# One decoder layer on one core: a raw transposed copy of x kept in DRAM from the first stage, inverse roots in pairs, and two smaller edits

## The chip, the cores and the metric

The kernel runs on one core of a Trainium2 chip. The metric is the device time of one execution in microseconds (us), taken as the median of repeated runs; the profile is one further execution with the hardware profiler on, and has a time of its own.

## The reference, cut to what matters

One layer of a hybrid decoder is computed for 1024 prompt tokens and 8 sampled tokens (T = 1032 rows in all, tiled as 8 tiles of 128 rows and a ninth of 8). What the change touches is the first norm and projection, the residual, and the one-token update of the delta state of the sampled tokens:

```
xn = rms_norm(x, norm_mix);  h = xn @ w_in          # first stage: norm, then projections
...
x = x + jnp.sum(gates * proj, axis=2) @ w_out       # x here is the raw input: the residual
hn = rms_norm(x, norm_ffn); ...
# sampled tokens (one step), per head and request:
S = exp(g) * (I - beta k k^T) S + beta k v^T        # an outer product is added to S
```

## The kernel before, in words

Everything is done in one launch, by five engines with queues of their own: TensorE (PE), VectorE (DVE), ScalarE (ACT), GpSimd (POOL) and SyncE (SP), which issues nearly all transfers in order. A scheduling layer sets the order in which instructions of independent steps are written to each engine; it is fixed at build time.

Large float32 products are made of three passes over operands split into a high part (`hi`, a rounded copy made with ScalarE) and a low part (`lo`, source minus high part, made with VectorE by `split`, lines 187 and 188); `mm3` and lines 163 to 165 are those passes, 128x344 or 128x296 each.

**First stage** (`p0_p1`). `p0(i)` loads row tile i of x (`x`, or a part of the tile `S`), squares it with ScalarE (L361), works out the inverse root of the mean with eleven small VectorE instructions over one column (L362, L196 to L200), scales the tile in place (L365), transposes it in two halves of four 128x128 blocks into PSUM tiles `tp` (two buffers, L370), and splits them into `xhi` and `xlo`. `weights` loads the indexer's columns of w_in in eight pieces, into five raw buffers, three of them parts of `S`; the high part is made with ScalarE (L302), the low part with GpSimd (L303), into `wB` and `wA`. `rawab` fills eight more columns of `wB`. `idx_proj(i)` multiplies a tile by `wB` and (from tile 2 on) `wA`; `scores(i)` follows, and its relu (L414) alternates between two halves of the tile `gr`, called `self.relu`. `z_out` puts other projections (`wraw`, `whi`, `wlo`) between.

**Sampled tokens' state** (`sample_delta`), interleaved with the projections that run beside the prompt's attention: eight times a matmul (L1495) makes four outer products at once, from `skv` (32 rows: the keys) and `sum` (32 x 512: the values masked by an identity), and VectorE adds them to states (L1498).

**Residual** (`x_T`). For `w_out` the kernel needs raw x with its columns on the partitions. `x_T(half)` loads half of x again, tile by tile, into two halves of `self.stage` (named `rs`), transposes it (L1512, 36 blocks a half) and copies it with ScalarE into `x2h[half]` (L1513). The scheduler has spread these over the stage in which `merge_b` and `merge_a` (products `pj<-o` and `pj<-oa`) and the sampled tokens' attention (`tq<-kvg`, L1389, on rows gathered by GpSimd's transfers) run.

Of the kernel before, what the change touches and what calls it, by code (L numbers as in the profile page):

```python
# [9 lines left out]
F32 = mybir.dt.float32  # L10
F32R = mybir.dt.float32r
BF = mybir.dt.bfloat16
F16 = mybir.dt.float16
I32 = mybir.dt.int32
AF = mybir.ActivationFunctionType
# [5 lines left out]
T = 1032  # L21
NT = 9
# [7 lines left out]
def rows_of(i):  # L30
    return (128 * i, 128 if i < 8 else 8)
# [23 lines left out]
class K:  # L55
# [218 lines left out]
    def p0_p1(self):  # L274
        nc, I, O, wk = self.nc, self.I, self.O, self.wk
        self.xhi = self.xp.tile([128, 8, T], F32R, name="xhi")
        self.xlo = self.xp.tile([128, 8, T], F32R, name="xlo")
        t = self.sp.tile([128, 2048], F32, name="gr", tag="kvb", bufs=1)
        self.gmix, self.relu, self.relu_n = t[:, 0:1024], t[:, 1024:2048], 0
        self.S = self.sp.tile([128, 4224], F32, name="S", bufs=1)  # L280
        self.soff = {i: 128 * (sum(range(3, i + 1))) for i in range(2, 8)}
        self.ik2 = self.wk.tile([128, 2, 1024], F32R, name="ik2", bufs=1)
        self.iqs = self.cp.tile([8, 576], F32, name="iqs", bufs=1)
        w = I['w_in'][0].rearrange("(k p) n -> p k n", p=128)
        wA = [wk.tile([128, 8, 296], F32R, name=f"wA{e}", bufs=1) for e in range(2)]
        wB = [wk.tile([128, 8, 296], F32R, name=f"wB{e}", bufs=1) for e in range(2)]

        raws = 0

        def weights(hl, c0, c1):  # L290
            nonlocal raws
            hi, lo = hl
            for k in range(0, 8, 2):
                if raws == 1:
                    self.xs[1] = self.x_load(1)
                j = raws % 5
                raws += 1
                raw = self.S[:, 592 * j:592 * j + 592] if j < 3 else wk.tile([128, 592], F32, name="raw2", tag="raw2", bufs=2)
                raw = raw[:, 0:2 * (c1 - c0)].rearrange("p (k c) -> p k c", k=2)
                nc.sync.dma_start(raw, w[:, k:k + 2, c0:c1])  # L300
                h = hi[:, k:k + 2, 0:c1 - c0]
                nc.scalar.activation(h, raw, AF.Copy)  # L302
                nc.gpsimd.tensor_tensor(lo[:, k:k + 2, 0:c1 - c0], raw, h.bitcast(F32), op=ALU.subtract)  # L303
        self.p0(0)
        weights(wB, 1064, 1352)
        raw = wk.tile([128, 8, 8], F32, name="rawab", bufs=1)
        nc.sync.dma_start(raw, w[:, :, 2888:2896])
        self.split(wB[0][:, :, 288:296], wB[1][:, :, 288:296], raw)
        self.p0(1)
        nc.sync.dma_start(self.rope_t.rearrange("p a b c d -> p (a b c d)"), I['c_rope'])  # L310
        weights(wA, 768, 1064)
        for i in range(NT):
            if i + 2 < NT:
                self.p0(i + 2)
            if i < 8:
                self.idx_proj(i, wA, wB)
            if i == 7:
                self.idx_proj(8, wA, wB)
                self.delta_gates()
                self.decays()  # L320
                self.conv_consts()
            if 2 <= i < 8:
                self.scores(i)
            if i == 2:
                z = [self.wcols(I['w_in'][0], 2896 + 128 * m) for m in range(2)]
            if i in (2, 5, 8):
                for m in range(2):
                    self.z_out(m, z[m], i // 3)
        for m in range(2, 4):
            z = self.wcols(I['w_in'][0], 2896 + 128 * m)  # L330
            for c in range(NCH):
                self.z_out(m, z, c)
# [17 lines left out]

    xs = {}

    def p0(self, i):
        nc, I, wk = self.nc, self.I, self.wk
        r0, n = rows_of(i)
        x = self.xs.pop(i, None)
        if x is None:
            x = self.x_load(i)
        junk = self.fp.tile([128, T], F32, name="st", tag="st", bufs=1).bitcast(BF)[:, 0:1024]
        ss = wk.tile([128, 1], F32, name="ss", bufs=2)  # L360
        nc.scalar.activation(junk[:n], x[:n], AF.Square, accum_out=ss[:n])  # L361
        nc.vector.tensor_scalar(ss[:n], ss[:n], 1.0 / 1024, EPS, op0=ALU.mult, op1=ALU.add)  # L362
        rs = wk.tile([128, 1], F32, name="rs", bufs=2)
        self.rsqrt(rs[:n], ss[:n])
        nc.vector.scalar_tensor_tensor(x[:n], x[:n], rs[:n], self.gmix[:n], op0=ALU.mult, op1=ALU.mult)  # L365
        for half in range(2):
            p = self.ptr()
            for j in range(4):
                k = half * 4 + j
                nc.tensor.transpose(p[:, j, :n], x[:n, k * 128:(k + 1) * 128], self.ident[:n, :n])  # L370
            ks = slice(half * 4, half * 4 + 4)
            self.split(self.xhi[:, ks, r0:r0 + n], self.xlo[:, ks, r0:r0 + n], p[:, :, :n])

    def idx_proj(self, i, wA, wB):
        nc, wk, O = self.nc, self.wk, self.O
# [48 lines left out]
    def dram(self):  # L424
        dp = self.dp
        self.d_g = dp.tile([16, 128, T], F32, name="d_g")
        self.d_z = dp.tile([4, 128, T], F32, name="d_z")
        self.d_qT = dp.tile([4, 128, 1024], F32, name="d_qT")
        self.d_kT = dp.tile([4, 128, 1024], F32, name="d_kT")
        self.d_kn = dp.tile([1024, 512], F32, name="d_kn")  # L430
        self.d_vn = dp.tile([1024, 512], F32, name="d_vn")
        self.d_qk = dp.tile([128, 8, 4, 128], F32, name="d_qk")
        self.d_D = dp.tile([128, 8, 4, 128], F32, name="d_D")
        self.d_G = dp.tile([32, 128], F32, name="d_G")
        self.d_Bt = dp.tile([128, 8, 4, 128], F32, name="d_Bt")
        self.d_b = dp.tile([4, 8, 4, 32, 32], F32, name="d_b")
        self.d_u = dp.tile([4, 8, 4, 32, 32], F32, name="d_u")
        self.d_q = dp.tile([T, 512], F32, name="d_q")
        self.d_k = dp.tile([T, 128], F32, name="d_k")
        self.d_v = dp.tile([T, 128], F32, name="d_v")  # L440
        self.d_s = dp.tile([8, 6, 128], F32, name="d_s")
        self.d_y = dp.tile([8, 128, T], F32, name="d_y")
        self.d_ob = dp.tile([4, 128, T], F32, name="d_ob")
        self.d_x2 = dp.tile([8, 128, T], F32, name="d_x2")
        self.d_act = dp.tile([22, 128, T], F32, name="d_act")
        self.d_oa = dp.tile([8, 64, 1024], F32, name="d_oa")
# [956 lines left out]
    def sample_delta(self):  # L1403
# [3 lines left out]
        def sm(name, shape=(128, 32)):  # L1407
            return wk.tile(list(shape), F32, name=name, bufs=1)
# [67 lines left out]
        nc.tensor.matmul(p[:, 0:32], self.ones, qk, start=True, stop=True)  # L1476
        nc.tensor.transpose(p[:32, 128:256], kr, self.ident)
        nc.tensor.transpose(p[:32, 256:384], kS, self.ident)
        kv = sm("skv", (32, 2, 128))
        nc.vector.tensor_copy(flat(kv), p[:32, 128:384])  # L1480
        nc.vector.tensor_scalar(be, p[:, 0:32], 1.0 / 128, EPS, op0=ALU.mult, op1=ALU.add)
        self.rsqrt(rq, be, t=rt[:, 0:32])
        tt(o, o, rq, op=ALU.mult)
# [2 lines left out]
        for h in range(4):  # L1486
            for half in range(2):
                c, b0 = 8 * h + 4 * half, 4 * half
                S0 = load_S(h, b0)
                um = wk.tile([32, 4, 128], F32, name="sum", tag="sum", bufs=1)  # L1490
                tt(um, kv[:, 1:2, :].to_broadcast([32, 4, 128]),
                   self.ident[:32, c:c + 4, None].to_broadcast([32, 4, 128]), op=ALU.mult)
                yield
                p = self.ptq()
                nc.tensor.matmul(flat(p), kv[:, 0], flat(um), start=True, stop=True)  # L1495
                for j in range(4):
                    sj = S0[:, j]
                    nc.vector.scalar_tensor_tensor(sj, sj, C[:, 96 + c + j:97 + c + j], p[:, j, :], op0=ALU.mult, op1=ALU.add)  # L1498
                nc.sync.dma_start(O['delta_s'][0, b0:b0 + 4, h].rearrange("b k v -> k b v"), S0)


    def x_T(self, half):

        nc, I = self.nc, self.I
        for i in range(NT):
            r0, n = rows_of(i)
            cs = slice(512 * half, 512 * half + 512)
            x = self.stage[:, 512 * (i % 2):512 * (i % 2) + 512]
            nc.sync.dma_start(x[:n], I['x_prompt'][0, r0:r0 + n, cs] if i < 8 else I['x_sample'][:, 0, cs])
            p = self.ptr()  # L1510
            for j in range(4):
                nc.tensor.transpose(p[:, j, :n], x[:n, 128 * j:128 * j + 128], self.ident[:n, :n])  # L1512
            nc.scalar.activation(self.x2h[half][:, :, r0:r0 + n], p[:, :, :n], AF.Copy)  # L1513

    def w45(self):
        nc, I, O = self.nc, self.I, self.O
# [315 lines left out]
```

## Time and profile before

| what | value |
|---|---|
| median of 3 runs | 1805.31 us (1805.31 to 1814.39) |
| the profiled execution | 1802.74 us, its span 1801.0 us, granted clock 0.995 |
| PE busy | 97% of the span |
| DVE, ACT, POOL busy | 67%, 47%, 2% |
| what ended last, by engine | PE 83%, DMA 7%, DVE 5%, ACT 3%, issue 2% |

The span runs from the first to the last instruction; the profiled execution's time has 1.7 us more around it. A busy TensorE row counts an instruction as busy while it is in the pipeline, so the pitch from one start to the next, not an instruction's own duration, is what it costs.

### The profile page before, as it was taken

Reading aid. Unit: us, or ns where it says so; the run is one execution under the profiler, and the core shown is the slowest. Engines: PE = TensorE matmul, PEld = TensorE weight load, DVE = VectorE, ACT = ScalarE, POOL = GpSimd, SP = SyncE. Lnnn points to the kernel's source line nnn. Section 1 sums busy time; section 2 is a strip of 40 time slices with the busy share of each in tenths; the row PEclk is TensorE's granted clock in tenths of the full one; section 3 lists DMA queues with packets and bytes.
Section 4 is the critical chain, followed back from the end, with each engine's and each line's share of the span. In section 5 each row is a group of like instructions: output and inputs, shape, how many; then the busy total and the mean of one; then the engine's idle time right before and its main releaser. Section 6 shows DMA issues by size and latency. Waiting matters only on the chain.

```text
span 1801.0 us, 31724 instructions
## 1 busy us (share of the span) xinstructions
PE 1740.0 (97%) x12276; PEld 1662.6 (92%) x12276; DVE 1210.6 (67%) x2776; ACT 852.1 (47%) x1575; POOL 42.2 (2%) x68
## 2 busy tenths in 40 slices
PE   5998999999999999999999999999999999999998
PEld 5998989999999988878899998999999999999998
DVE  7775558999899777797656477766666665733222
ACT  4567467877845345687444243433333333412012
POOL 3001100000000000000000000000000000000000
PEclk9999999999999999999999999999999999999999
DMA  6115434434546543254567434322222323732122
GB/s 194 43 35 153 130 101 145 130 113 120 159 131 167 149 137 109 84 183 141 195 235 226 138 110 135 101 81 85 82 72 75 91 72 125 223 100 73 51 80 69
DMA packets 293595, 218.01 MB, mean 121 GB/s; under 512 B 39292, under 2 KB 267456, under 8 KB 292412
## 3 DMA queue, kind: packets, MB, share of 16 engines
q1 hardware_dynamic: 291716, 205.50, 37.8%
q0 software_dynamic: 1728, 10.49, 1.7%
q8 instruction: 96, 1.57, 0.4%
q14 instruction: 55, 0.45, 0.1%
HBM read 154.17 MB, written 61.87 MB: 120 GB/s over the span
## 4 chain that ended last, share of the span: by engine, by line
PE 83%; DMA 7%; DVE 5%; ACT 3%; issue 2%; SPq 0%; ACTq 0%; DVEq 0%
PE pj L163 15%; PE pj L165 15%; PE pj L164 15%; PE A L1706 2%; PE A L1707 2%; PE A L1708 2%; PE D L1706 2%; PE F L1706 2%; PE F L1707 2%; PE D L1707 2%; PE F L1708 2%; PE D L1708 2%; PE PT L1055 1%; DMA araw<-d_act 1%; PE B L1706 1%
## 5 line engine op out<-in xcount | busy, mean ns | idle before, releaser
L163 PE MATMUL pj<-xhi,whi 128*128 128x344 f32 x912 | 297.5, 326 | 5.3 <-ACT gs L862 4.3
L165 PE MATMUL pj<-xhi,wlo 128*128 128x344 f32 x912 | 294.3, 323 | 0.0
L164 PE MATMUL pj<-xlo,whi 128*128 128x344 f32 x912 | 293.3, 322 | 0.0
L187 ACT ACTIVATE whi<-wraw 128x1024 fp32r<-128x1024 f32 (+4 forms) x126 | 115.2, 914 | 249.4 <-PE pj L164 208.0
L163 PEld LDWEIGHTS pj<-xhi,whi 128*128 128x128 f32 x912 | 171.9, 189 | 9.3 <-ACT gs L862 5.7
L164 PEld LDWEIGHTS pj<-xlo,whi 128*128 128x128 f32 x912 | 171.9, 188 | 2.0 <-issue 1.1
L165 PEld LDWEIGHTS pj<-xhi,wlo 128*128 128x128 f32 x912 | 171.9, 188 | 1.4
L164 PE MATMUL pj<-act,whi 128*128 128x344 f32 x528 | 170.3, 323 | 0.7 <-DVE act L188 0.7
L165 PE MATMUL pj<-act,wlo 128*128 128x344 f32 x528 | 168.9, 320 | 0.8 <-DVE wlo L188 0.8
L163 PE MATMUL pj<-act,whi 128*128 128x344 f32 x528 | 169.3, 322 | 0.2 <-DVE x L1768 0.2
L188 DVE TENSOR_TENSOR wlo<-wraw,whi 128x1024 fp32r<-128x1024 f32 (+3 forms) x104 | 116.2, 1118 | 54.4 <-ACT whi L187 52.7
L1768 DVE TENSOR_TENSOR x<-pj,x 128x344 f32<-128x344 f32 x96 | 48.5, 514 | 140.0 <-PE pj L165 139.9
L768 DVE TENSOR_SCALAR_CACHE_REDUCE kvb<-S,cand 128x384 bf16<-128x384 f32 (+3 forms) x128 | 103.7, 810 | 2.0
L165 PEld LDWEIGHTS pj<-act,wlo 128*128 128x128 f32 x528 | 99.2, 188 | 1.5 <-DVE wlo L188 1.3
L164 PEld LDWEIGHTS pj<-act,whi 128*128 128x128 f32 x528 | 99.2, 188 | 1.0 <-DVE act L188 1.0
L163 PEld LDWEIGHTS pj<-act,whi 128*128 128x128 f32 x528 | 99.2, 188 | 0.9 <-issue 0.4
L1706 PE MATMUL D<-hb,wx 128*128 128x258 f32 x328 | 93.0, 284 | 2.0 <-DVE E L1729 2.0
L1708 PE MATMUL D<-hb,wx 128*128 128x258 f32 x328 | 92.7, 282 | 0.7 <-DVE wx L188 0.7
L1706 PE MATMUL A<-hb,wlo 128*128 128x258 f32 x328 | 93.0, 283 | 0.0
L1707 PE MATMUL A<-hb,wlo 128*128 128x258 f32 x328 | 92.8, 283 | 0.0
L1708 PE MATMUL A<-hb,wlo 128*128 128x258 f32 x328 | 92.8, 283 | 0.0
L1707 PE MATMUL D<-hb,wx 128*128 128x258 f32 x328 | 92.6, 282 | 0.0
(587 smaller groups left out, 4790.3 us busy)
## 6 DMA issues: line engine op xcount, KB each, us to landing
wraw<-in_w_gate_up SPq DMA_DIRECT2D x50, 512.0 KB
wraw<-in_w_in SPq DMA_DIRECT2D x38, 512.0 KB
d_act<-x SPq DMA_DIRECT2D x41, 258.0 KB
araw<-d_act SPq DMA_DIRECT2D x20, 516.0 KB
d_g<-gs SPq DMA_DIRECT2D x48, 172.0 KB
wraw<-in_w_out SPq DMA_DIRECT2D x16, 512.0 KB
wraw<-in_w_branch SPq DMA_DIRECT2D x12, 512.0 KB
wraw<-in_w_down SPq DMA_DIRECT2D x16, 384.0 KB
```

What stands on the lines that cost most here:

```text
L163: nc.tensor.matmul(ps, lh, rh, start=(j == 0), stop=False)
L164: nc.tensor.matmul(ps, lh, rl, start=False, stop=False)
L165: nc.tensor.matmul(ps, ll, rh, start=False, stop=(j == last))
L187: self.nc.scalar.activation(hi, src, AF.Copy)
L188: self.nc.vector.tensor_tensor(lo, src, hi.bitcast(F32), op=ALU.subtract)
L768: nc.vector.tensor_scalar(junk[:r, :n], s, thr[:r, j:j + 1], 0.0, op0=ALU.is_lt, op1=ALU.add, accum_out=cnt[:r, j:j + 1])
L1055: nc.tensor.transpose(p[:, j, :], P[j][:, 128 * s:128 * s + 128], self.ident)
L1706: nc.tensor.matmul(p, lh, rh, start=(first and k == 0), stop=False, skip_group_check=True)
L1707: nc.tensor.matmul(p, lh, rl, start=False, stop=False, skip_group_check=True)
L1708: nc.tensor.matmul(p, ll, rh, start=False, stop=(k == 3), skip_group_check=True)
L1768: nc.vector.tensor_tensor(xv, p, xv, op=ALU.add)
```

## The change

1. In the first stage each tile of x is also transposed raw: 8 more transposes, two ScalarE copies out of PSUM into the halves of `self.relu`, and two transfers of 128 x 4 x 128 to a DRAM tensor `d_xT` (256 KB each, in pieces of 512 bytes). 18 copies and 18 transfers in all.
2. `x_T(half)` becomes one transfer of `d_xT` into `x2h[half]` (2.1 MB, pieces of 4128 bytes).
3. From tile 2 on, `p0` takes two tiles at a time, so that the small root instructions run over two columns once instead of over one column twice.
4. The low parts of the eight weight pieces are made with VectorE instead of GpSimd.
5. The outer products' operands are spread over 128 rows as float32r: high and low parts of the keys and of the values in the four combinations of 32 rows each, so that one pass of 128 rows replaces a float32 product over 32 rows. Eight more small ScalarE and VectorE instructions and a small table `eye4` prepare them once.

```diff
-                nc.gpsimd.tensor_tensor(lo[:, k:k + 2, 0:c1 - c0], raw, h.bitcast(F32), op=ALU.subtract)
+                nc.vector.tensor_tensor(lo[:, k:k + 2, 0:c1 - c0], raw, h.bitcast(F32), op=ALU.subtract)
...
-            if i + 2 < NT:
-                self.p0(i + 2)
+            if i % 2 == 0 and i + 2 < NT:
+                self.p0(*range(i + 2, min(i + 4, NT)))
...
+    def p0(self, *tiles):
+        xs, ss = [], wk.tile([128, 2], F32, name="ss", bufs=2)
+        rs = wk.tile([128, 2], F32, name="rs", bufs=2)
+        for a, i in enumerate(tiles):
...
+            nc.scalar.activation(junk[:n], x[:n], AF.Square, accum_out=ss[:n, a:a + 1])
+            for half in range(2):
+                p = self.x_transposed(x, i, half)
+                t = self.relu[:, 512 * self.relu_n:512 * self.relu_n + 512].rearrange("p (j t) -> p j t", j=4)[:, :, :n]
+                self.relu_n = 1 - self.relu_n
+                nc.scalar.activation(t, p, AF.Copy)
+                nc.sync.dma_start(self.d_xT[4 * half:4 * half + 4, :, 128 * i:128 * i + n].rearrange("j p t -> p j t"), t)
+        nc.vector.tensor_scalar(ss[:n, :c], ss[:n, :c], 1.0 / 1024, EPS, op0=ALU.mult, op1=ALU.add)
+        self.rsqrt(rs[:n, :c], ss[:n, :c])
+        for a, i in enumerate(tiles):
+            x, t = xs[a], slice(128 * i, 128 * i + n)
+            nc.vector.scalar_tensor_tensor(x[:n], x[:n], rs[:n, a:a + 1], self.gmix[:n], op0=ALU.mult, op1=ALU.mult)
+            for half in range(2):
+                ks = slice(half * 4, half * 4 + 4)
+                self.split(self.xhi[:, ks, t], self.xlo[:, ks, t], self.x_transposed(x, i, half))
...
-        kv = sm("skv", (32, 2, 128))
-        nc.vector.tensor_copy(flat(kv), p[:32, 128:384])
+        for a in range(4):
+            r = slice(32 * a, 32 * a + 32)
+            nc.vector.tensor_copy(eye[r], self.ident[0:32, 0:32])
+            for x, src, low in ((k4, kq4[0], a // 2), (v4, kq4[1], a % 2)):
+                if low:
+                    nc.vector.tensor_tensor(x[r], src, x[0:32].bitcast(F32), op=ALU.subtract)
+                else:
+                    nc.scalar.activation(x[r], src, AF.Copy)
...
-                um = wk.tile([32, 4, 128], F32, name="sum", tag="sum", bufs=1)
+                um = wk.tile([128, 4, 128], F32R, name="sum", tag="sum", bufs=1)
...
-                nc.tensor.matmul(flat(p), kv[:, 0], flat(um), start=True, stop=True)
+                nc.tensor.matmul(flat(p), k4, flat(um), start=True, stop=True)
...
     def x_T(self, half):
-        for i in range(NT):
...
+        self.nc.sync.dma_start(self.x2h[half], self.d_xT[4 * half:4 * half + 4].rearrange("j p t -> p j t"))
```

Three places show how the order moves. The first is VectorE at the start, where tile 0's root (`rst`, `rs`) ends and tile 1's begins; before:

```order
15 L199 SCALAR_TENSOR_TENSOR rst<-rst,ss 128x1
16 L200 SCALAR_TENSOR_TENSOR rs<-rst,rs 128x1
17 L365 SCALAR_TENSOR_TENSOR x<-x,rs,gr 128x1024
18 L362 TENSOR_SCALAR ss<-ss 128x1
19 L196 TENSOR_SCALAR rs<-ss 128x1
```

and now:

```order
15 L199 SCALAR_TENSOR_TENSOR rst<-rst,ss 128x1
16 L303 TENSOR_TENSOR wB_124<-S,wB_123 128x2x288
17 L200 SCALAR_TENSOR_TENSOR rs<-rst,rs 128x1
18 L377 SCALAR_TENSOR_TENSOR x<-x,rs,gr 128x1024
19 L373 TENSOR_SCALAR ss<-ss 128x1
20 L303 TENSOR_TENSOR wB_124<-S,wB_123 128x2x288
21 L196 TENSOR_SCALAR rs<-ss 128x1
22 L303 TENSOR_TENSOR wB_124<-S,wB_123 128x2x288
23 L198 TENSOR_TENSOR rst<-rs 128x1
24 L303 TENSOR_TENSOR wB_124<-raw_184,wB_123 128x2x288
```

The first low part of a weight piece now stands ahead of the last step of tile 0's root, and the other three between the steps of tile 1's. The second place is SP's queue of transfers in the first stage, from the load of tile 4 (`x`) on, now:

```order
20 L346 DMA x<-in_x_prompt 128x1024
21 L1226 DMA pt<-in_page_table 128x1x1 x3
22 L372 DMA d_xT<-gr 128x4x128
...
27 L372 DMA d_xT<-gr 128x4x128
28 L346 DMA x<-in_x_prompt 128x1024
29 L409 DMA out_ik_p<-nat 128x64
30 L139 DMA wraw<-in_w_in 128x8x128 x2
31 L372 DMA d_xT<-gr 128x4x128 x2
32 L409 DMA out_ik_p<-nat 128x64
33 L372 DMA d_xT<-gr 128x4x128 x5
```

and ScalarE's queue that goes with it (L371 is the copy of a raw half tile, L366 the square, L400 the copy of a projection):

```order
25 L366 ACTIVATE st,ss<-x 128x1024
26 L371 ACTIVATE gr<-tp 128x512 x2
27 L400 ACTIVATE nat<-pj 128x296
28 L366 ACTIVATE st,ss<-x 128x1024
29 L187 ACTIVATE ik_119<-tq 128x128
30 L371 ACTIVATE gr<-tp 128x512 x2
31 L187 ACTIVATE xhi<-tp 128x4x128 x4
```

The writes of tile 1 are SP's rows 22 and 27, those of tile 2 row 31, behind two loads into `wraw`; ScalarE's row 26 is the raw tile 2, row 30 the raw tile 3, and the high parts of the normalized tiles 2 and 3 (row 31) come behind it. The third place is TensorE where the sampled tokens' attention meets the merges; before:

```order
4274 L1379 MATMUL tq<-ident,sPn 8x64
4275 L163 MATMUL pj<-oa_10242,whi 128x344
4276 L164 MATMUL pj<-oa_10243,whi 128x344
4277 L165 MATMUL pj<-oa_10242,wlo 128x344
4278 L163 MATMUL pj<-oa_10244,whi 128x344
4279 L1385 MATMUL tq<-sv,Pd 16x128
4280 L1389 MATMUL tq<-kvg,kTp 16x128 x16
```

and now:

```order
4261 L1396 MATMUL tq<-ident,sPn 8x64
4262 L1402 MATMUL tq<-sv,Pd 16x128
4263 L1406 MATMUL tq<-kvg,kTp 16x128 x16
...
4268 L1402 MATMUL tq<-sv,Pd 16x128
4269 L1406 MATMUL tq<-kvg,kTp 16x128 x16
4270 L163 MATMUL pj<-o_9540,whi 128x344
```

All four groups of the gathered rows now run first, then the last 36 matmuls of `merge_b`, then `merge_a`. In SP's queue both transfers of `x_T` stand there together, ahead of the loads for it:

```order
362 L896 DMA d_y<-gt 128x1032
363 L1530 DMA x_10212<-d_xT 128x4x1032
364 L1530 DMA x_10277<-d_xT 128x4x1032
365 L1555 DMA gf<-in_norm_ffn 128x8x1
366 L154 DMA wraw<-in_w_branch 128x4x256
367 L891 DMA gt<-d_g 128x1032
```

Before, the first two of the 18 small loads of `x_T` stood at that place, behind the same write of `d_y`, and the other 16 were spread over the merges. Outside these two stretches (the first stage, and from the end of the prompt's attention to `w_out`) no engine's order differs.

## Rows read from the trace of the kernel before

**Rows 1.** The page: span, and busy time with its share of the span.
```profile
span 1801.0 us, 31724 instructions
PE 1740.0 (97%) x12276; PEld 1662.6 (92%) x12276; DVE 1210.6 (67%) x2776; ACT 852.1 (47%) x1575; POOL 42.2 (2%) x68
```

**Rows 2.** Windows of the first stage: busy time by engine, granted clock, DMA share, GB/s.
```profile
0.00:25.00 25.00, 10.06 (x50) 9.37 (x50) 16.64 (x51) 13.13 (x22) 9.00 (x19) 1.00 0.85 272
...
100.00:125.00 25.00, 25.00 (x174) 22.54 (x173) 17.85 (x53) 15.13 (x34) 0.29 (x1) 1.00 0.02 4
```

**Rows 3.** Timeline of PE, start and duration, with [idle before <-releaser].
```profile
8.88 1.94 PE L370 MATMUL tp<-ident,x 128*128 128x128 f32 x8 [8.88 <-DVE x L365]
...
17.49 0.58 PE L164 MATMUL pj<-wB,xhi 128*128 128x296 f32 x1 [4.26 <-DVE rs L200]
...
32.84 0.61 PE L165 MATMUL pj<-wA,xlo 128*128 128x296 f32 x1 [3.70 <-DVE xlo L188]
```

**Rows 4.** Timeline of DVE in the same stretch.
```profile
10.77 0.16 DVE L199 SCALAR_TENSOR_TENSOR rst<-rst,ss 128x1 f32<-128x1 f32 x1
10.97 1.27 DVE L200 SCALAR_TENSOR_TENSOR rs<-rst,rs 128x1 f32<-128x1 f32 x1
...
17.13 0.22 DVE L188 TENSOR_TENSOR wB<-rawab,wB 128x64 fp32r<-128x64 f32 x1
```

**Rows 5.** Timeline of POOL.
```profile
10.82 2.76 POOL L303 TENSOR_TENSOR wB<-S,wB 128x576 fp32r<-128x576 f32 x2 [0.82 <-ACT wB L302]
```

**Rows 6.** Line 188 in 0 to 60 us: ns (min/median/max), first and last start.
```profile
L188 DVE TENSOR_TENSOR xlo<-tp,xhi x13: 677/683/693, 16.5 to 59.6; 128x512 fp32r<-128x512 f32 x13
```

**Rows 7.** Timeline of SP: issue of transfers.
```profile
25.54 5.58 SPq L139 DMA_DIRECT2D wraw<-in_w_in  x2
```

**Rows 8.** The chain that ended last, 0 to 150 us: start, duration, what.
```profile
140.07 1.37 DMA d_G<-nat
...
141.89 7.30 DMA x<-d_G
```

**Rows 9.** Timeline of PE round one outer product.
```profile
673.89 0.32 PE L165 MATMUL pj<-xhi,wlo 128*128 128x344 f32 x1
674.14 1.12 PE L1495 MATMUL tq<-sum,skv 32*128 32x512 f32 x2
675.20 0.50 PE L1059 MATMUL PV<-ph,v 128*128 128x512 f32 x1
675.53 0.39 PE L1023 MATMUL PT<-k,q 128*128 128x512 f32 x1
675.76 0.39 PE L1024 MATMUL PT<-k,q 128*128 128x512 f32 x1
```

**Rows 10.** Window of the outer products.
```profile
680.00:700.00 20.00, 20.00 (x114) 17.10 (x113) 14.32 (x35) 10.37 (x20) 0.00 (x0) 1.00 0.40 117
```

**Rows 11.** Timeline of PE in the stage of x_T.
```profile
928.96 0.33 PE L165 MATMUL pj<-oa,wlo 128*128 128x344 f32 x1
929.12 0.60 PE L1512 MATMUL tp<-ident,rs 128*128 128x128 f32 x4
929.48 0.40 PE L163 MATMUL pj<-oa,whi 128*128 128x344 f32 x1
929.72 0.60 PE L1512 MATMUL tp<-ident,rs 128*128 128x128 f32 x4
...
972.34 0.63 PE L1512 MATMUL tp<-ident,rs 128*128 128x128 f32 x4 [1.54 <-ACT x L1513]
```

**Rows 12.** Line 1513: durations in ns (min/median/max), first and last start.
```profile
L1513 ACT ACTIVATE x<-tp x18: 198/594/600, 924.5 to 981.9; 128x512 f32<-128x512 f32 x16, 128x32 f32<-128x32 f32 x2
```

**Rows 13.** Windows after the end of the prompt's attention.
```profile
890.00:900.00 10.00, 7.95 (x56) 6.36 (x55) 6.25 (x13) 1.82 (x3) 0.00 (x0) 0.97 0.52 195
900.00:910.00 10.00, 10.00 (x77) 7.64 (x75) 2.89 (x6) 2.81 (x6) 0.94 (x1) 0.86 1.00 363
```

**Rows 14.** Timeline of PE: one group of gathered rows.
```profile
915.80 3.67 PE L1389 MATMUL tq<-kvg,kTp 128*16 128x128 f32 x32
```

More of the change, by code (lines that the diff above doesn't have):

```diff
@@ L351 @@
     xs = {}
[L353 to L372, printed above, removed]
+    def p0(self, *tiles):
+        nc, wk = self.nc, self.wk
+        c = len(tiles)
+        xs, ss = [], wk.tile([128, 2], F32, name="ss", bufs=2)
+        rs = wk.tile([128, 2], F32, name="rs", bufs=2)
+        n = rows_of(tiles[0])[1]
+        for a, i in enumerate(tiles):
+            x = self.xs.pop(i, None)
+            if x is None:
+                x = self.x_load(i)
+            xs.append(x)
+            junk = self.fp.tile([128, T], F32, name="st", tag="st", bufs=1).bitcast(BF)[:, 0:1024]
+            nc.scalar.activation(junk[:n], x[:n], AF.Square, accum_out=ss[:n, a:a + 1])
[13 more added lines that the diff above has]
+                self.split(self.xhi[:, ks, t], self.xlo[:, ks, t], self.x_transposed(x, i, half))
@@ L374, in idx_proj, with x_transposed @@
+    def x_transposed(self, x, i, half):
+        n = rows_of(i)[1]
+        p = self.ptr()
+        for j in range(4):
+            k = half * 4 + j
+            self.nc.tensor.transpose(p[:, j, :n], x[:n, k * 128:(k + 1) * 128], self.ident[:n, :n])
+        return p[:, :, :n]
     def idx_proj(self, i, wA, wB):
@@ L443, in dram @@
         self.d_ob = dp.tile([4, 128, T], F32, name="d_ob")
+        self.d_xT = dp.tile([8, 128, T], F32, name="d_xT")
         self.d_x2 = dp.tile([8, 128, T], F32, name="d_x2")
@@ L1478, in sample_delta @@
         nc.tensor.transpose(p[:32, 256:384], kS, self.ident)
-        kv = sm("skv", (32, 2, 128))
-        nc.vector.tensor_copy(flat(kv), p[:32, 128:384])
+        kq4 = [p[:32, 128 * j:128 * j + 128] for j in (1, 2)]
+        k4, v4 = (wk.tile([128, 128], F32R, name=x, bufs=1) for x in ("sk4", "sv4"))
+        eye = wk.tile([128, 32], F32, name="eye4", bufs=1)
+        for a in range(4):
[6 more added lines that the diff above has]
+                    nc.scalar.activation(x[r], src, AF.Copy)
         nc.vector.tensor_scalar(be, p[:, 0:32], 1.0 / 128, EPS, op0=ALU.mult, op1=ALU.add)
@@ L1489, in sample_delta @@
                 S0 = load_S(h, b0)
-                um = wk.tile([32, 4, 128], F32, name="sum", tag="sum", bufs=1)
-                tt(um, kv[:, 1:2, :].to_broadcast([32, 4, 128]),
-                   self.ident[:32, c:c + 4, None].to_broadcast([32, 4, 128]), op=ALU.mult)
+                um = wk.tile([128, 4, 128], F32R, name="sum", tag="sum", bufs=1)
+                tt(um, v4[:, None, :].bitcast(F32).to_broadcast([128, 4, 128]),
+                   eye[:, c:c + 4, None].to_broadcast([128, 4, 128]), op=ALU.mult)
                 yield
                 p = self.ptq()
-                nc.tensor.matmul(flat(p), kv[:, 0], flat(um), start=True, stop=True)
+                nc.tensor.matmul(flat(p), k4, flat(um), start=True, stop=True)
                 for j in range(4):
@@ L1502, in x_T @@
     def x_T(self, half):
-        nc, I = self.nc, self.I
-        for i in range(NT):
[L1506 to L1513, printed above, removed]
+        self.nc.sync.dma_start(self.x2h[half], self.d_xT[4 * half:4 * half + 4].rearrange("j p t -> p j t"))
     def w45(self):
```

## The prediction, on record before the change was run

> **What bounds the kernel now.** The page comes first: TensorE is busy 1740.0 of 1801.0 us, VectorE two thirds of it and GpSimd 2% [rows 1]. So an edit counts by the TensorE time that it takes out or puts in, and by the few waits that TensorE still has. The windows say where these are: in the first 25 us TensorE works 10.06 us while the transfers are 85% busy; by 100 to 125 us it works 25.00 of 25.00 [rows 2]. The timeline names the waits: 8.88 us before the first transpose, 4.26 us at 17.49 and 3.70 us at 32.84, the last for `xlo` of tile 2 [rows 3]. The wait at 17.49 is put down to a root step (L200), but a projection does not read roots; the last piece of `wB` that it needs is the low part from `rawab`, which VectorE makes at 17.13 to 17.35, behind those root steps [rows 4]. One of these takes 0.16 us alone and 1.27 us at 10.97, and just then, from 10.82, GpSimd makes a low part [rows 4, 5].
>
> The two later places of the change are full. Around the outer products TensorE is busy 20.00 of 20.00 us [rows 10], so what is cut from it there shortens the run. In the stage of `x_T` the same holds, with small holes (7.95 of 10 in 890 to 900) [rows 13].
>
> **Outer products.** One costs 674.14 to 675.20, 1.06 us, and it disturbs its neighbours: the projection before it starts 0.25 us ahead where 0.16 is usual [rows 9, 11], and the matmul behind it takes 0.33 to the next start where a one-pass matmul of 512 columns takes 0.23 (675.53 to 675.76) [rows 9]. Together 1.06 + 0.09 + 0.10 = 1.25 us. Now it is one pass of 512 columns, 0.23, with little or no disturbance: 1.0 us less, eight times: **−8.1 us**. Bounds: 8 × 0.8 = −6.6, if the disturbance stays; nothing, if the additions on VectorE set the pace (a rival below). The eight small instructions that spread the operands run once, on engines with a quarter of the window free or more [rows 10]; without that cover they would cost some 8 × 0.2 = 1.6 us, by the 0.22 us of a small VectorE instruction [rows 4].
>
> **x_T's transposes.** A group of four takes 929.12 to 929.48, 0.36 us, and the matmul behind it 0.24 in place of 0.16: 0.44 us [rows 11]. There were 18 groups: **−7.9 us**. The wait of 1.54 us at 972.34, for ScalarE's copy out of PSUM, goes with them: **−1.5 us** [rows 11]. The 18 copies at 594 ns are off ScalarE there [rows 12].
>
> **Raw transposes in the first stage.** The same 18 groups come back early. Those of tiles 0 to 3 (8 groups) fall where TensorE idles [rows 2, 3]; uncovered they would be 8 × 0.44 = 3.5 us more. Those of tiles 4 to 8 (10 groups) stand among projections: 10 × 0.44 = **+4.4 us**.
>
> **The start.** GpSimd's low parts move to VectorE. A low part of 512 columns takes 0.68 us there [rows 6], so one of 576 to 592 about 0.75, against a mean of 1.38 us on GpSimd (2.76 for two) [rows 5], and nothing stretches the root steps. `wB` is complete about 3 us earlier; I put TensorE's restart at 14.6 instead of 17.49. That alone is no gain, because TensorE then runs into the next wait, for tile 2. There a new chain is late. Each raw half tile is copied into one of two halves of `relu`, so the copies of tile 3 wait until the writes of tile 2 have landed. In SP's order these writes stand behind two loads into `wraw`, whose issue took from 25.54 to 31.12 [rows 7]. And in ScalarE's order the copies of tile 3 stand ahead of `xhi` of tiles 2 and 3. So what is queued behind the waiting copy is just what TensorE needs.
>
> How long such a write takes no row shows. From below: a small write to `d_G` took 1.37 us; from above: the read of the same tensor, with larger pieces and more bytes, took 7.30 [rows 8]. I take 2.3 us: the 1.37, and 256 KB at about 300 GB/s (windows show 272 and 363 [rows 2, 13]), 0.9. Then: 31.1 + 2.3 = 33.4, two copies of 0.59 [rows 12] to 34.6, one half of `xhi` of about the same length to 35.2, against 32.84 now [rows 3]; and four matmuls that ran before the old wait, 0.16 each, come behind the new one. 2.4 + 0.6 = **+3.0 us**, +2.1 with the landing at 1.37 and +8.0 with 7.30. Pairing the roots saves three times eleven small instructions on VectorE, 0.16 us each; it hides under TensorE, and its price is that tile 2 waits for tile 3's square, which the raw copies hold up anyway.
>
> Later the same two buffers are wanted by the pairs 4 and 5, 6 and 7, and by the relus of the scores. TensorE is full there, so most waits are covered; I take **+1.0 us** for all three, nothing from below.
>
> The Trainium skill, page "DMA: Bandwidth & Descriptors", section "Anatomy of one DMA — SWDGE (gpsimd) path", speaks against this part, though of transfers that GpSimd issues: one has a fixed cost of about 2.0 us, most of it the receipt of the write, and is slowest to complete with HBM as the target. By it a write of 256 KB would land after 2.0 + 0.6 = 2.6 us (an estimate), and the sum would be some 1 us worse over four places; the 1.37 us of the write in rows 8 is already under that fixed cost, and the sum goes by the row.
>
> **The loads of `x2h`.** Two transfers, 4.2 MB, now stand together at about 882 us, ahead of the loads that the merges want. At 363 GB/s, as in 900 to 910 [rows 13], they fill 11.6 us. Before, the transfer engines were 52% and 100% busy in 890 to 910 [rows 13], so the loads behind are late. What covers it: TensorE now runs four groups of gathered rows at 3.67 us [rows 14] before it comes to `merge_a`, 14.7 us of work that wants none of those loads, and 36 matmuls of `merge_b`. I cost it at nothing; the ends are −2 (the holes in 890 to 900 [rows 13] close) and +6 (half of 11.6 uncovered).
>
> **The sum.** −8.1 − 7.9 − 1.5 + 4.4 + 3.0 + 1.0 = −9.1 us. The profiled execution took 1802.7, its span 1801.0 and 1.7 around it, and would take 1793.6. The runs' median, 1805.3, is 2.6 above it; on that scale the forecast is **1796.2 us**. Its own range, from the terms' ends, is 1791 to 1801. The change gains in two places that are full and pays in one that is full and in one that waits.
>
> **Rivals.**
>
> *The start is not late.* The issue of the `wraw` loads is long because the second waits for a buffer that VectorE empties. With unstretched root steps it might come 4 to 5 us earlier, and then the wait at 32.84 shrinks by 2 instead of growing by 3, and the waits on `relu` vanish: −8.1 − 7.9 − 1.5 + 4.4 − 2.0 = −15.1, **1790 us**. For it: 4.26 us of wait lay behind the stretch [rows 3, 4, 5]. Against it: VectorE gets 8 × 0.75 = 6 us more to do in just that stretch.
>
> *The jam at 882.* The 4.2 MB hold back the gathered rows as well, which GpSimd's transfers bring, and then nothing covers: +4 to +5, **1801 us**. For it: the share of 1.00 in 900 to 910 [rows 13]. Against: the four groups need not come at once.
>
> *The outer products are not on the path.* If VectorE's additions set when the next step may run, the 8.1 us turn into waits: −1.0, **1804 us**. Against: TensorE has no hole in that window and VectorE has 14.32 of 20 [rows 10].
>
> *Slower: the writes land late.* If a write in pieces of 512 bytes takes nearer 7.3 us than 2.3 [rows 8], every one of the four places (tiles 2 and 3, 4 and 5, 6 and 7, the scores) can pay the difference, since ScalarE waits in order and the high parts are behind it. From 2.3 + 9.1 / 4 = 4.6 us on the gain is gone; at 7.3 it is +20 − 9.1 = +10.9, **1816 us**. For it: that stage moves 272 GB/s already [rows 2]. Against: after 100 us the share is 0.02, and only the first place lies in the crowd.
>
> **How the numbers follow.** Forecast 0.50, start not late 0.17, jam 0.15, outer products off the path 0.10, writes late 0.08. A measurement of this kernel tells about 0.5%, 9 us, from no change; −9.1 sits on that line, so I give half of the forecast to either side: faster 0.25 + 0.17 + 0.02 = 0.44; same 0.25 + 0.15 + 0.10 = 0.50, less that 0.02 and with 0.02 of late writes that only cancel the gain: 0.50; slower 0.06. The range takes in the first rival with the outer ends of its terms (−18) and the third with +1.5: 1787 to 1807, leaving out the late writes and a tail of the rest.
>
> **What the profile would show.** Right: the outer product as one row with a pitch of 0.23 to 0.3; no transposes in 924 to 982; TensorE at its restart before 15 us, then a wait of several us that ends near 35 and is put down to `xhi` or `xlo`, with ScalarE's copies held by the landing of `d_xT`; landings of 2 to 3 us; the groups of gathered rows back to back. Wrong: landings over 4.6 us, a wait ahead of `merge_a` put down to `wraw` or `gt`, or waits at the outer products that end with VectorE.

## The result, and the profile after

The changed kernel is slower: 1840.34 us median (1833.58 to 1842.94, 6 runs) against 1806.16 (6 runs), ratio 1.0169 with a 95% interval of 1.0142 to 1.0197: some 30 us by the ratio, 34 by the medians. The forecast was 1796.2 within 1787 to 1807. The page of the changed kernel, span and busy time, against [rows 1]:

```profile
span 1839.0 us, 31691 instructions
PE 1757.5 (96%) x12268; PEld 1680.0 (91%) x12268; DVE 1203.0 (65%) x2758; ACT 852.0 (46%) x1577; POOL 30.3 (2%) x60
```

The span grew by 38.0 us. TensorE idles 81.5 us (1839.0 − 1757.5) where it idled 61.0, 20.5 more. It is also busy 17.5 us longer, with 72 transposes in one place instead of another and about 8 us less of outer products. Most of the rest is clock: the mean granted clock, 0.995 before, is 0.979 now. Since it has two levels, 1.2 and 2.4 GHz, that is (1 − 0.979) × 1839 × 2 = 77 us at the lower one, and was (1 − 0.995) × 1801 × 2 = 18. Both leave out the span's start: the kernel before has a granted clock of 1.00 in 0 to 25 us [rows 2], yet its projections there stand 0.25 us apart, the pitch that the rows below have at the lower level:

```profile
17.87 0.45 PE L165 MATMUL pj<-wB,xlo 128*128 128x296 f32 x1
18.12 0.45 PE L163 MATMUL pj<-wB,xhi 128*128 128x296 f32 x1
```

To see where, I cut the span at the first start of four instructions that every kernel of this study has: the transposes `pi<-ident,Ub` (the delta rule's inverse), the products `tq<-skq` (the sampled tokens' state), the transposes `tq<-ident,sP` of 64x64 (the weights of their attention; four small ones of 8x8, over 100 us earlier, have the same name) and `pj<-ident,nr` (the second norm). The five lengths, in us, from the profiled executions:

```
                       I first   II delta  III prompt   IV merges,  V the   span
                       stage ..   rule     attention     w_out      rest
before                  451.3     198.7     242.1        143.4      765.5   1801.0
after                   476.5     200.1     235.6        157.4      769.4   1839.0
e1 outer products       448.7     202.6     233.4        144.6      766.2   1795.6
e2 low parts            448.5     199.6     242.0        142.6      767.1   1799.8
e3 pairs                451.7     200.1     246.8        144.5      763.9   1807.0
e4 raw copies           463.9     215.7*    236.1*       157.8      765.9   1839.3
e5 own buffers          470.6     215.7*    231.3*       161.8      768.0   1847.3
e6 spread loads         475.8     201.5     231.5        156.0      768.8   1833.5
e7 copies alone         475.2     202.1     234.2        144.9      765.6   1822.0
e8 loads alone          453.6     215.1*    226.5*       163.8      763.3   1822.4
e9 outer + low parts    451.2     198.7     236.8        144.2      769.3   1800.2
e11 tied groups         476.1     199.3     242.5        142.1      767.7   1827.8
e12 no writes           464.5     202.4     233.7        145.2      766.7   1812.6
e13 ScalarE's queue     472.5     215.3*    228.1*       157.9      766.4   1840.2
```

The change loses 25.2 us in I and 14.0 in IV, gains 6.5 in III. (The star is a second order of the delta rule's work, told under e8.) Each row is one execution, and code that is the same differs too: V, which no edit touches, lies between 763.3 and 769.4, III of e3 is 4.7 longer than before, I of e1 2.6 shorter. So a few us in one stage decide nothing. The border between III and IV also moves: 24 matmuls of `merge_b`, 4 us of work, went from III to IV in the changed kernel.

**The first stage.** TensorE's timeline, stretches with waits, against [rows 3]:

```profile
14.74 0.59 PE L164 MATMUL pj<-wB,xhi 128*128 128x296 f32 x1
...
30.68 0.66 PE L387 MATMUL tp<-ident,S 128*128 128x128 f32 x4 [1.77 <-ACT gr L371]
33.59 0.65 PE L387 MATMUL tp<-ident,S 128*128 128x128 f32 x4 [2.25 <-ACT gr L371]
...
38.82 2.06 PE L387 MATMUL tp<-ident,S 128*128 128x128 f32 x8 [2.38 <-ACT gr L371]
40.62 0.61 PE L163 MATMUL pj<-wA,xhi 128*128 128x296 f32 x1
...
44.11 0.45 PE L165 MATMUL pj<-wA,xlo 128*128 128x296 f32 x1
44.35 0.42 PE L163 MATMUL pj<-wA,xhi 128*128 128x296 f32 x1
44.60 0.30 PE L164 MATMUL pj<-wA,xhi 128*128 128x296 f32 x1
44.74 0.30 PE L165 MATMUL pj<-wA,xlo 128*128 128x296 f32 x1
```

The first projection goes on at 14.74 (forecast 14.6), but tile 2's begins at 40.62 (forecast 35.2; before, the wait for tile 2 ended at 32.84 [rows 3]). The waits name ScalarE's raw copies. And after them TensorE runs at the lower clock: 0.24 to 0.25 us from start to start up to 44.60, 0.14 from there. ScalarE's timeline, its copies, and what they wait for:

```profile
15.17 0.60 ACT L371 ACTIVATE gr<-tp 128x512 f32<-128x512 f32 x1 [0.89 <-PE tp L387]
...
18.38 0.60 ACT L371 ACTIVATE gr<-tp 128x512 f32<-128x512 f32 x1 [0.52 <-PE tp L387]
...
30.03 0.60 ACT L371 ACTIVATE gr<-tp 128x512 f32<-128x512 f32 x1 [1.92 <-DMA d_xT<-gr]
32.94 0.60 ACT L371 ACTIVATE gr<-tp 128x512 f32<-128x512 f32 x1 [2.31 <-DMA d_xT<-gr]
...
38.17 0.60 ACT L371 ACTIVATE gr<-tp 128x512 f32<-128x512 f32 x1 [1.41 <-DMA d_xT<-gr]
```

and SP's, the issue of the writes that they wait for:

```profile
23.19 0.54 SPq L372 DMA_DIRECT2D d_xT<-gr  x1
...
27.30 0.38 SPq L372 DMA_DIRECT2D d_xT<-gr  x1
...
30.01 1.40 SPq L139 DMA_DIRECT2D wraw<-in_w_in  x2
31.50 3.34 SPq L372 DMA_DIRECT2D d_xT<-gr  x2
```

Tile 1's first copy is done at 15.77; its write is issued at 23.19, 7.4 us later, behind other entries of SP; it gives the buffer back at 30.03, 6.8 us after the start of the issue. The second: 18.98, 27.30 (8.3 later), 32.94 (5.6). The first of the pair at 31.50 releases at 38.17 (6.7). So a write of 256 KB took 5.6 to 6.8 us from the start of its issue, where I had put 2.3.

The Trainium skill, page "DMA: Bandwidth & Descriptors", section "Anatomy of one DMA — SWDGE (gpsimd) path", gives 2.0 us fixed and a rate by which such a write lands after 2.6 (an estimate, from a path other than this one). The trace disagrees, more than twofold, in a stretch where the transfers are 71% busy (0 to 50 us).

Tile 2 is about half of the stage's loss. Counting TensorE's matmuls without these transposes (`tp`), the 500th starts 13.4 us later than before (118.0 against 104.6 us), the 1000th 24.6 later (220.9 against 196.3). In between stands a wait that the kernel before hasn't got (its longest after 105 us is 2.11); TensorE's row, and ScalarE's ahead of it:

```profile
198.04 0.54 PE L163 MATMUL pj<-xhi,whi 128*128 128x344 f32 x1 [4.39 <-ACT gs L337]
```

```profile
195.16 1.06 ACT L564 ACTIVATE x<-x 128x1024 f32<-128x1024 f32 x1 [5.38 <-POOL x L562]
```

ScalarE, which works in order, waits there for a tile of decays that GpSimd masks, and the copy of a projection (`gs`) comes behind it. The same wait is 2.70 us in e12, without the writes, and 3.58 in e4; why the raw copies bring it about, no run tests. In all of stage I TensorE idles only 4.3 us more than before (33.6 against 29.2). The 72 transposes are 7.9 us by the price of [rows 11], and the lower clock, granted for 24 us more of this stage (30.6 against 6.8), accounts for at most 11 (24 × 0.11 / 0.25, by the pitch 0.25 for 0.14).

**The merges.** SP's timeline, the entries that matter:

```profile
901.97 1.52 SPq L1530 DMA_DIRECT2D x<-d_xT  x2
...
920.40 0.80 SPq L974 DMA_DIRECT2D rs<-d_oa  x2
941.89 0.32 SPq L896 DMA_DIRECT2D d_y<-gt  x1
...
944.02 0.45 SPq L974 DMA_DIRECT2D rs<-d_oa  x1
...
963.21 0.79 SPq L909 DMA_DIRECT2D gt<-d_g  x2
```

and TensorE's waits there:

```profile
935.38 0.42 PE L163 MATMUL pj<-o,whi 128*128 128x344 f32 x1 [0.77 <-DVE soS L1409]
942.69 0.43 PE L163 MATMUL pj<-oa,whi 128*128 128x344 f32 x1 [1.02 <-ACT oa L187]
...
949.32 1.38 PE L163 MATMUL pj<-oa,whi 128*128 128x344 f32 x3 [4.27 <-ACT oa L187]
968.63 0.42 PE L163 MATMUL pj<-oa,whi 128*128 128x344 f32 x1 [1.44 <-DVE gt L914]
...
987.97 0.43 PE L163 MATMUL pj<-oa,whi 128*128 128x344 f32 x1 [2.36 <-DVE gt L914]
999.81 0.43 PE L163 MATMUL pj<-oa,whi 128*128 128x344 f32 x1 [3.97 <-DVE gt L914]
```

From 921 to 942 SP issues nothing. It stands at the write of `d_y`, which wants the last product of `merge_b`; that product, the 36 matmuls from 935.38, now comes behind the four groups of gathered rows. All of `merge_a`'s loads but the two at 920.40 are behind the write, and `merge_a`, now in one block, waits for one load after another: 6.2 us in three waits for `oa`, up to 949, then 9.1 us in four for `gt`, up to 1000. The later loads of `gt` (963.21) are issued long after the write; there it also counts that nothing else stands between `merge_a`'s steps.

### The profile page after: what moved, and what is told of

Its sections match the earlier page's. It is cut to its first block, busy times and chain, and to the rows that moved or that the text cites. A ratio compares the mean times of both kernels' runs of the same rounds, so it can differ in the third digit from the quotient of the medians.

```text
span 1839.0 us, 31691 instructions
## 1 busy us (share of the span) xinstructions
PE 1757.5 (96%) x12268; PEld 1680.0 (91%) x12268; DVE 1203.0 (65%) x2758; ACT 852.0 (46%) x1577; POOL 30.3 (2%) x60
## 4 chain that ended last, share of the span: by engine, by line
PE 85%; DMA 7%; DVE 4%; ACT 2%; issue 1%; SPq 0%; DVEq 0%; ACTq 0%
PE pj L163 15%; PE pj L165 15%; PE pj L164 15%; PE A L1724 2%; PE A L1723 2%; PE A L1725 2%; PE D L1723 2%; PE F L1723 2%; PE F L1724 2%; PE D L1724 2%; PE F L1725 2%; PE D L1725 2%; PE PT L1072 2%; PE B L1723 1%; DMA gt<-d_g 1%
```

## The experiments

**e1, outer products alone.** The kernel before with the change's edits to `sample_delta`:

```diff
-                nc.tensor.matmul(flat(p), kv[:, 0], flat(um), start=True, stop=True)
+                nc.tensor.matmul(flat(p), k4, flat(um), start=True, stop=True)
```

> The kernel before with only the outer products over 128 rows. Theory A (the loss comes from the first stage and from the loads of x2h; the outer products gained what the sum said): 6 to 9 us faster than the kernel before. Rival (they are not on the path, or the clock falls there because of them): within 2 us of it, or slower.

Ratio 0.9966 (0.9944 to 0.9987): 6 us faster. Stage III shows it without the rest: 242.1 to 233.4, −8.7, of which about 1.1 is seven matmuls of `merge_b` that went to IV. The timeline round one outer product, against [rows 9]:

```profile
683.82 0.32 PE L165 MATMUL pj<-xhi,wlo 128*128 128x344 f32 x1
683.98 0.40 PE L1504 MATMUL tq<-sum,sk 128*128 128x512 f32 x1
684.21 0.40 PE L1060 MATMUL PV<-pl,v 128*128 128x512 f32 x1
684.44 0.39 PE L1059 MATMUL PV<-ph,v 128*128 128x512 f32 x1
```

0.23 us, no disturbance on either side: 1.25 − 0.23, eight times, as the sum had it.

**e2, low parts alone.** `nc.gpsimd.tensor_tensor` to `nc.vector.tensor_tensor` in `weights`, nothing else.

> The kernel before with only the weights' low parts on VectorE. Theory A (the raw copies and their writes make the first stage late): 0 to 4 us faster. Rival B (6 us more on VectorE in the first 25 us make it late): 8 us slower or more.

Ratio 0.9977 (0.9962 to 0.9992): 4 us faster (1 to 7), as A said. Stage I is 2.8 us shorter, but in e1, which leaves it alone, it is 2.6 shorter, and in e9, with the same low parts, as long as before: the total shows the gain, the stage doesn't.

**e3, roots in pairs alone.** `p0(*tiles)` without the raw copies.

> The kernel before with only the inverse roots in pairs, without raw copies. Theory A: within 4 us of the kernel before. Rival B (taking two tiles together is what delays tile 2): 8 us slower or more.

Ratio 0.9998 (0.9980 to 1.0015). Pairs alone cost nothing and give nothing beyond some 3 us of noise.

**e4, raw copies alone.** Copies, writes and loads from `d_xT`; the roots one tile at a time.

> The kernel before with only the raw copies of x to DRAM and x2h read from there, the roots one tile at a time, the low parts on GpSimd. Theory A (writes that hold ScalarE in the first stage, and 4.2 MB of loads ahead of those of the merges): 25 to 45 us slower. Rival B: no more than 5 us slower.

Ratio 1.0179 (1.0156 to 1.0201): 32 us slower, as expected, but not by the same sum as the changed kernel: I loses 12.6 here, half of what it loses there, IV 14.4, and the rest is in II, where this kernel has the starred order. Stage I is 11.3 us shorter than with pairs (e7), although the low parts are on GpSimd. In ScalarE's order the high parts of tile 2 stand ahead of the raw copies of tile 3 here, and tile 2's projection begins at 36.33, not at 40.62.

**e5, two more buffers.** The changed kernel; raw copies of odd tiles from 3 on in the weight pieces' buffers:

```diff
-                t = self.relu[:, 512 * self.relu_n:512 * self.relu_n + 512].rearrange(...)[:, :, :n]
+                if i > 1 and i % 2:
+                    t = wk.tile([128, 592], F32, name="raw2", tag="raw2", bufs=2)[:, 0:512]
```

> The changed kernel, with the raw copies of tiles 3, 5 and 7 put into two other buffers (those of the weight pieces, free by then) and not into the halves of relu. Theory A1 (the first stage is late because ScalarE's copies wait for writes that have not landed): 8 us or more faster than the changed kernel. Rival A2 (the transposes themselves, the order and the low clock after them are the loss): within 4 us of the changed kernel.

Ratio 1.0196 (1.0165 to 1.0228), no faster than the changed kernel: by the total, A2. But the stages disagree with the total: I is 5.9 us shorter, less than A1's 8, and the starred order in II and a longer IV take it back. ScalarE's timeline:

```profile
28.73 0.60 ACT L375 ACTIVATE gr<-tp 128x512 f32<-128x512 f32 x1 [1.75 <-DMA d_xT<-gr]
31.89 0.60 ACT L375 ACTIVATE gr<-tp 128x512 f32<-128x512 f32 x1 [2.55 <-DMA d_xT<-gr]
32.68 0.60 ACT L375 ACTIVATE raw<-tp 128x512 f32<-128x512 f32 x1
```

Tile 3's copy (`raw`) no longer waits; tile 2's still do, for tile 1's writes. That leaves A1 open, so e12 takes the writes away.

**e6, the loads spread.**

```diff
+            if c0 == 0:
+                x = self.x2h[m // 4][:, m % 4]
+                nc.vector.tensor_copy(x[:, 0:1], yhi[:, m, 0:1].bitcast(F32))
+                nc.sync.dma_start(x, self.d_xT[m])
```

> The changed kernel, with the two loads of x2h cut into eight, one behind each step of merge_a's first pass (a small copy on VectorE ties each to its step). Theory A (4.2 MB together ahead of the merges' loads are the loss there): 6 to 14 us faster than the changed kernel. Rival (the order of TensorE's work is the loss, which stays): within 3 us of it.

Ratio 1.0157 (1.0124 to 1.0190) to before, where the changed kernel has 1.0169. The medians lie 6 us apart, the lower end of A, but of the 5.5 between the two spans IV has 1.4, and III, which the edit doesn't touch, 4.2. So 4.2 MB in one place were not the loss. SP's timeline suggests what is, and e11 tests it:

```profile
910.16 27.43 SPq L896 DMA_DIRECT2D d_y<-gt  x2
```

**e7, raw copies written but not used.** The changed kernel with `x_T` as before.

> The changed kernel with the raw copies written in the first stage but not used: x_T loads and transposes x as before. The loss of the first stage alone, with the gains of the outer products and of the low parts. Theory A (both places lose; the first stage about 20 us): 8 to 20 us slower than the kernel before. Rival C (the merges alone lose): within 4 us of the kernel before, or faster.

Ratio 1.0120 (1.0089 to 1.0151): 21 us slower, just above A's range and far from C: I as long as in the changed kernel, IV as before.

**e8, the loads alone.** The changed kernel without the six lines of the raw copies; `x_T` reads `self.d_g[4 * half:4 * half + 4]`.

> The changed kernel without raw copies in the first stage; the two loads of x2h read rows of the gates' tensor in place of x (same size and pieces, so the residual adds another tensor). The loss of the merges alone. Theory A (both places lose; the merges some 13 us against a work saving of 9): within 6 us of the kernel before. Rival D (the first stage alone loses, the loads are harmless): 15 to 20 us faster than the kernel before, the whole sum of outer products, low parts and x_T.

Ratio 1.0095 (1.0063 to 1.0128): 17 us slower, outside both expectations. IV loses here too, and more than the 13 us expected (+20.5); I is about as long as before (453.6). What nobody expected is II, +16.5. Two orders of the delta rule's stage occur among these kernels, and this one has the other: the matmuls of one line in II, between the first and second of my marks, kernel before and e8,

```profile
L163 PE MATMUL pj<-xhi,whi 128*128 128x344 f32 x232 | 76.9, 331 | 2.4 <-ACT gs L862 2.4
```

```profile
L163 PE MATMUL pj<-xhi,whi 128*128 128x344 f32 x247 | 81.8, 331 | 6.8 <-ACT gs L873 6.8
```

15 more of these, with their two partners 45 matmuls of 0.16 us, 7 us that left stage III, and longer waits. So the star costs about 16 − 7 = 9 us. The scheduling layer chose it in e4, e5, e8 and e13, with and without raw copies, and not in the changed kernel. Without it e8 would be some 8 us slower than before, nearer to A; that IV loses 6 us more here than in the changed kernel stays open.

**e9, the two parts that gained.**

> The kernel before with the two parts that gained alone: the outer products over 128 rows and the low parts on VectorE. If they add up: 8 to 12 us faster than the kernel before. If they don't (one takes the other's cover): no faster than either alone, 4 to 6 us.

1796.11 us, ratio 0.9940 (0.9921 to 0.9959): 11 us faster than before, and over 40 faster than the changed kernel. They add up (0.9966 × 0.9977 = 0.9943).

**e11, the groups tied behind merge_b.** The changed kernel with

```diff
+        self.tie = self.wk.tile([8, 1], F32, name="tie", bufs=1)
+        nc.vector.tensor_scalar(self.tie, y[:8, T - 1:T], 0.0, 1.0, op0=ALU.mult, op1=ALU.add)
...
+        nc.vector.tensor_scalar(Pd, Pd, self.tie, None, op0=ALU.mult)
...
-        weave(islice(self.sample, 33), 25, islice(steps, BESIDE), BESIDE)
+        weave(islice(self.sample, 30), 25, islice(steps, BESIDE), BESIDE)
```

> The changed kernel, with the four groups of gathered rows tied behind merge_b's last product (their weights are multiplied by a one that is made from it), so that the write of d_y, which stands in SP's queue ahead of merge_a's loads, no longer waits for them. Theory E (that write held the queue, and merge_a came late for it): 8 to 15 us faster than the changed kernel. Rival F (the 4.2 MB of loads are the loss): within 3 us of it.

Ratio 1.0073 (1.0051 to 1.0095); 1819.22 against 1840.34 us: 17 us faster than the changed kernel by the ratios, 21 by the medians, more than E's 15. IV falls from 157.4 to 142.1, with the same number of matmuls in it (975 and 974): TensorE idles there 9.7 us for 22.3. (The profiled execution, 1829.5 us, lies above the median: it is 6.9 us longer in III, where its clock is low, as the end of this document shows.) SP's timeline:

```profile
907.70 1.31 SPq L1533 DMA_DIRECT2D x<-d_xT  x2
...
910.43 8.85 SPq L154 DMA_DIRECT2D wraw<-in_w_branch  x1
...
926.09 0.81 SPq L976 DMA_DIRECT2D rs<-d_oa  x2
928.38 0.32 SPq L896 DMA_DIRECT2D d_y<-gt  x1
```

The two loads of `x2h` still stand ahead, and the load of weights behind them still takes 8.85 us to issue. The write of `d_y` no longer holds the queue, and F is out. But the tie also puts the groups back between `merge_a`'s steps, and with the waits for `oa` those for `gt` are gone. So the 15 us belong to the order of the groups; how much of it is the held queue (the 6.2 us of waits for `oa` point there) and how much the cover that `merge_a` lost, no run divides.

**e12, no writes.** e7 without the line of L372.

> The changed kernel with raw transposes and copies of them in the first stage, but no writes of the copies; x_T loads and transposes x as before. Beside the run that also writes them (e7_copies, 1826.7 us). Theory A1 (writes in SP's queue and their landings make the first stage late): 10 us or more faster than e7_copies. Rival A2 (the transposes, copies and the order of the pairs do): within 4 us of e7_copies.

Ratio 1.0049 (1.0025 to 1.0073); 1814.27 against 1826.73 us, 12.5 faster than e7. I is 464.5 against 475.2. TensorE's timeline, tile 2:

```profile
31.79 0.66 PE L386 MATMUL tp<-ident,S 128*128 128x128 f32 x4 [3.07 <-ACT gr L371]
32.98 1.94 PE L386 MATMUL tp<-ident,S 128*128 128x128 f32 x8 [0.54 <-DVE rst L198]
34.76 0.61 PE L163 MATMUL pj<-wA,xhi 128*128 128x296 f32 x1
```

A1 for 10.7 us of stage I. What is left, 464.5 against 451.2 in e9, 13.3 us, is the raw transposes and copies, where I had 4.4, in the order that the pairs give them; e9 has single roots. A run with raw copies, single roots and no writes is missing.

**e13, the writes issued by ScalarE.** `nc.sync.dma_start` to `nc.scalar.dma_start` in L372.

> The changed kernel, with the 18 writes of the raw copies issued by ScalarE itself and not by SP. The delta-rule stage comes out in the other of its two orders here, which cost some 15 us in the runs that had it, so the first part alone is compared: up to the first product of the delta-rule's inverse, 476.5 us in the changed kernel and 451.3 before. Theory G (about half of the wait of the raw copies is the place of the writes in SP's queue): 5 us or more shorter than 476.5. Rival H (the landing alone counts, or the issue now holds ScalarE): within 3 us of 476.5.

Stage I 472.5, 4.0 shorter: between G and H, and not far above the 2.6 us by which this stage differs between before and e1, so the share of SP's queue stays open. The whole is 1.0195 (1.0156 to 1.0234), with the star (whose 15 us in the expectation are stage II alone; less what leaves III it is about 9).

## Why the prediction was wrong

- **Outer products, −8.1.** Right: −8.7 in its stage (about −7.6 without the matmuls that left it), −6 (−10 to −2) by the ratio of e1. With it the rival "not on the path" is out.
- **x_T's transposes, −7.9, and its wait, −1.5.** The work went, but the stage it left became 14.0 us longer. The step that failed is "I cost it at nothing": I let the four groups of gathered rows cover late loads. They were work ahead of `merge_b`'s last product, that product feeds a write, the write stands in SP's queue, and behind it stand the loads of `merge_a`. I had the rows of both queues and did not follow that write. Put behind it again, the groups gave IV 15.3 us back (e11). Waits ahead of `merge_a`'s matmuls that are put down to `gt` were named as a sign of being wrong, and came. The rival "the jam at 882" had the right stage and the wrong cause (e6, e11).
- **Raw transposes, +4.4.** Mis-sized: 13.3 us by e12 against e9, with the order of the pairs in it. All 18 groups by the price of [rows 11] are 7.9. At the 500th matmul that is not one of these transposes (104.9 us in e9, 112.2 in e12) e12 is 7.3 us behind, with 16 groups done, about their whole price, so the eight early groups were hardly hidden; the other 6 come between there and 210 us, where two groups are left, and I can't divide them between order, the wait at 198 us and clock.
- **The start, +3.0, and relu's buffers, +1.0.** The chain was right (writes behind other entries of SP, copies of tile 3 behind them, high parts behind the copies), its sizes were not: 5.6 to 6.8 us of landing for 2.3 (over 4.6 was a sign of being wrong), and 7.4 to 8.3 us in SP's queue already for tile 1, where I had looked at tile 2 alone. The writes cost 10.7 us of stage I (e7 against e12). The range's end for the landing, 7.3, was near the truth; I chose the low end for a write into a crowd of transfers.
- **"Its price is that tile 2 waits for tile 3's square, which the raw copies hold up anyway."** Wrong: the raw copies of tile 3 are in tile 2's way only because of the pairs. Single roots are 11.3 us faster in stage I (e4 against e7), and without raw copies pairs are free (e3). These 11.3 and the 10.7 of the writes are in part the same wait and don't add up: with single roots, copies and writes together cost stage I 12.6 (e4 against before), with pairs 25.2.
- **Low parts.** Right in kind: no loss, 4 us faster (e2). The restart at 14.74 was forecast. The rival "the start is not late" wanted the loads of `wraw` 4 to 5 us earlier; their issue ended at 31.41, where it had ended at 31.12.
- **The clock** was in no term. 77 − 18 = 59 us more at 1.2 GHz, at 0.25 us in place of 0.14 a matmul, lose at most 59 × 0.11 / 0.25 = 26 us, which agrees with the page of the profile: 17.5 us more busy with 8 us less work. That it falls behind waits is what the rows show (35 to 44 us above); that fewer waits bring it back whole is not shown, since it also varies from run to run. The Trainium skill, page "TensorE: Matmul & The Clock Gate", section "Part 1: The HAM clock gate (the "warmup" mystery)", calls the lower clock the default, a throttle that activity releases. The stretch at 35 to 44 us agrees with it; the window of e11 at the end of this document does not, if busy time is the activity.
- **The rival that ended slower**, late writes, was the right mechanism for about a third of the loss (10.7 of 34 us); I gave it 0.08.

## What to carry to other kernels

Where a change reorders work, look in each in-order queue for a write that wants the work which was put back, and count the loads behind it: here 15 us came from work that was put ahead of one such write, and not from the 4.2 MB beside it. A copy that must leave through a transfer costs its place in the queue and its landing before the buffer is free, and both are to be priced from the busy stretch it falls into. In a kernel that is bound by TensorE, a new wait can be paid twice, once as idle time and again at the lower clock behind it (stage IV: 22.3 us idle and about 18 at the lower clock in the changed kernel, 9.7 and 3 in e11); and a total can hide a gain when the scheduler turns another stage round, so compare stage by stage.

## What the runs showed of the hardware that was not expected

The clock can stay low while TensorE is busy throughout. In the profile of e11, the window 685 to 695 us (busy time of PE, PEld, DVE, ACT, POOL, then the granted clock, DMA share, GB/s):

```profile
685.00:695.00 10.00, 10.00 (x40) 9.04 (x38) 5.03 (x14) 4.74 (x9) 0.00 (x0) 0.50 0.27 79
```

The sampled tokens' state products run there: 26 of the 40 matmuls are `tq<-skq` of 128x2, two columns each, so a row that counts as busy can stream very little. The pitch rises at 678 us, just behind 16 more of them. The same work in the kernel before had 1.00 in 650 to 670 us. No wait stands in that window, so what brings the clock down there stays open.
